# One decoder layer on one core: six pairs of weight columns multiplied by a seven-product scheme, and one projection moved

## The chip, the core and the metric

The kernel runs on one core of a Trainium2 chip. A core has TensorE (matrix products), VectorE (DVE in the profile), ScalarE (ACT), GpSimd (POOL) and SyncE (SP, which here only issues transfers). Each engine works through its own instructions in order, and engines wait for one another on semaphores. The metric is the device time of one launch, in microseconds (us).

## The reference

One layer of a hybrid decoder: 256 tokens, model width 2048, all in float32. Cut to its products:

```python
hn = rmsnorm(h, norm_mix_w)                       # h is x, (256, 2048)
q, k, v, g_ret, xr, yr, g_a, g_b = split(hn @ w_in)
ret_out = silu(g_ret) * head_groupnorm(chunkwise_retention(rotary(q), rotary(k), v))
rnn_out = gelu(yr) * rg_lru(causal_dwconv(xr))
merged = sigmoid(g_a) * (ret_out @ w_proj_ret) + sigmoid(g_b) * (rnn_out @ w_proj_rnn)
h = h + merged @ w_mix_out
h = h + memory_cross_attention(rmsnorm(h), rmsnorm(mem), xa_w_q, xa_w_k, xa_w_v) @ xa_w_o
gate, val = split(causal_dwconv(rmsnorm(h) @ ffn_w_up))
h = h + (silu(gate) * val) @ ffn_w_down           # 5632 hidden features
return rmsnorm(h, final_norm_w)
```

The matrices of the mixers and of the attention are 2048 x 2048 each (`w_in` is 2048 x 14336), `ffn_w_up` is 2048 x 11264 and `ffn_w_down` 5632 x 2048.

## The kernel before

**Units.** Every dense product is cut into *units*. A unit is one piece of a weight, 1 MB: four k-tiles of 128 rows (`KC` = 4) by 512 columns (`BW` = 512). There are 356. `weight_plan` (L64) lists the products in the order in which they are computed, `weight_stream` (L89) lays the pieces of all weights one behind the other in memory in that order ("the wall"), and `prefetch` (L191) walks along it: SP loads the next piece into one of three `raw` buffers (L202), ScalarE copies it to a rounded half `hi` (L221), VectorE subtracts to get the rest `lo` (L222). `hi` and `lo` have three buffers each, and the splits are made two units ahead. The rounding type (fp32r) lets TensorE take the product of two float32 numbers as three matmuls: high by high, low by high, high by low.

**Two kinds of product.** `gemm_t` (L253, matmuls at L276) keeps the weights stationary and gives its result by feature. `gemm_n` (L290, matmuls at L286 to L288 in `products_n`) keeps the tokens' tiles stationary and gives its result by token: two tiles of 128 tokens, four k-tiles, three matmuls of 512 columns each, so 24 in a unit. Results go to three accumulators in PSUM, each two banks (128 x 1024 float32).

**Activations** are kept by feature as `[128, 2, 512]` tiles: two k-tiles, and for each 256 tokens of the high half and 256 of the low half. `split_pair` (L330) makes them (ScalarE L337, VectorE L338), `halves` (L306) takes them apart. They and most other large tiles come from one pool of 27 buffers of 4 KB a partition (`big`); `tmp` tiles come from a second pool of ten.

**The order of the work.** q, k, v and gate of the retention; four blocks of the recurrence (`recur` L623, loop from L656); `gated` (L686) for `w_proj_rnn` four times, then for `w_proj_ret` four times, where the two are added (L705), transposed and split into `merged` (`turn_merged` L698); `residual` (L714) for `w_mix_out`; attention (`attend` L808); `residual` for `xa_w_o`; the FFN in three parts of 4, 4 and 3 blocks of 512 hidden features. In each part, `conv_up` (L834) multiplies, convolves (ScalarE L840, VectorE L842) and stores gate and value, L909 to L912 make the activation and its split `hid`, and `down` (L847) multiplies with `ffn_w_down` and adds (L853).

`residual` takes four column blocks one after the other: `gemm_n`, one VectorE add of 128 x 1024 into the residual rows `hrow` (L721), squares for the next norm, and the transposes and splits of the new rows (`turn` L727). While it multiplies `w_mix_out`, `memory_steps` (L746) does the norm of the memory rows `mnat` between the blocks.

Small work that follows a product is put off with `later(n, ...)` (L232): it is issued n units after the present one, so that TensorE has weights to multiply meanwhile. On top of that a scheduler orders the instructions of each engine when the program is built; at run time the order is fixed.

```python
for k in range(0, nk, KC):
    prefetch(1)
    (r_, c_), parts = ahead.pop(0)
    ...
    prefetch(AHEAD)
    yield k, parts
    step[0] += 1
```

Of the kernel before, what the change touches and what calls it, by code (L numbers as in the profile page):

```python
# [16 lines left out]
P = 128  # L17
# [10 lines left out]
BW = 512  # L28
# [35 lines left out]
def weight_plan():  # L64

    w0 = "w_in"
    plan = []
    for g in range(2):
        for c in (O_Q, O_K):
            plan += [(w0, 0, NT, c + g * BW), (w0, 0, NT, O_V + g * 1024 + (c == O_K) * BW)]  # L70
        plan += [(w0, 0, NT, O_G + g * 1024 + b * BW) for b in range(2)]
    for b in range(4):
        plan += [(w0, 0, NT, c + b * BW) for c in (O_XR, O_YR)]
    for c, w in ((O_GB, "w_proj_rnn"), (O_GA, "w_proj_ret")):
        for b in range(4):
            plan += [(w0, 0, NT, c + b * BW), (w, 0, NT, b * BW)]
    plan += [("w_mix_out", 0, NT, b * BW) for b in range(4)]
    plan += [(w, 0, NT, b * BW) for b in range(4) for w in ("xa_w_k", "xa_w_q")]
    plan += [(w, 0, NT, b * BW) for w in ("xa_w_v", "xa_w_o") for b in range(4)]
    b0 = 0  # L80
    for nb_ in FF_PARTS:
        for b in range(b0, b0 + nb_):
            plan += [("ffn_w_up", 0, NT, c + b * BW) for c in (0, FF)]
        plan += [("ffn_w_down", b0 * BW, 4 * nb_, b * BW) for b in range(4)]
        b0 += nb_
    return plan


def weight_stream(inputs):  # L89

    out = []
    for name, row, nk, c in weight_plan():
        w = np.asarray(inputs[name])[0]
        for k in range(0, nk, KC):
            r = row + k * P
            out.append(w[r : r + KC * P, c : c + BW].reshape(KC, P, BW).transpose(1, 0, 2))
    return np.ascontiguousarray(np.stack(out))
# [3 lines left out]
def hybrid_layer(  # L101
# [20 lines left out]
    bp = ctx.enter_context(tc.tile_pool(name="bp", bufs=27))  # L122
# [54 lines left out]
    stream = [(row + k * P, c) for w, row, nk, c in plan for k in range(0, nk, KC)]  # L177
    assert len(stream) == wall.shape[0]
# [12 lines left out]
    def prefetch(n):  # L191
        while len(ahead) < n and taken[0] < len(stream):
            row, c = stream[taken[0]]
            src = wall[taken[0]]
# [31 lines left out]
            ahead.append(((row, c), parts))  # L226
# [9 lines left out]
    def chunks(nk, w, row, c):  # L236

        w_, row_, nk_, c_ = plan[gemms[0]]
        assert (row_, nk_, c_) == (row, nk, c) and w_ == w, (gemms[0], row, nk, c)
        gemms[0] += 1  # L240
        for k in range(0, nk, KC):
            prefetch(1)
            (r_, c_), parts = ahead.pop(0)
            assert (r_, c_) == (row + k * P, c)
            prefetch(AHEAD)
            yield k, parts
# [3 lines left out]
            for _, fn in due:  # L250
                fn()

# [37 lines left out]
    def gemm_n(w, row, st, nk, col):  # L290
# [8 lines left out]
        return a  # L299

# [129 lines left out]
    def rms(rows, pin=False):  # L430

        ss = sp_.tile([P, 2, 4], F32, tag="ss0", name=nm("ss"))
        for c in range(4):
            for tt in range(2):
                junk = tp.tile([P, BW], F32, tag="tmp", name=nm("junk"))
                i = act.activation(junk, rows[c][:, tt, :], AF.Square, accum_out=ss[:, tt, c : c + 1])
                if pin:
                    tc.keep_in_program_order(i)
# [217 lines left out]
    for b in range(4):  # L656
# [28 lines left out]

    def gated(c0, w, st, b, o):  # L686

        a = gemm_n("w_in", 0, xs, NT, c0 + b * BW)
        t = tp.tile([P, 2, BW], F32, tag="sig", bufs=2, name=nm("sig"))
# [6 lines left out]
    merged = []  # L696

    def turn_merged(m, pr):  # L698
        for t in transposed(m[:, :, pr * S : (pr + 1) * S]):
            merged.append(split_pair(t, 0.5))  # L700

    mb = [gated(O_GB, "w_proj_rnn", rnn, b, big([P, 2, BW], s="mb")) for b in range(4)]
    for b in range(4):
        m = gated(O_GA, "w_proj_ret", ret, b, big([P, 2, BW], s="m"))
# [6 lines left out]
    mnat = [load_rows(mem, c) for c in range(4)]  # L711
    ms = Pairs(mem_t, p_mem)

    def residual(w, st, out, wcol, steps=None):  # L714

        ss = sp_.tile([P, 2, 4], F32, tag="ss0", name=nm("ss"))
        for b in range(4):
            if steps:
                steps(b)
            h = hrow[b]  # L720
            dve.tensor_add(h, h, gemm_n(w, 0, st, NT, b * BW))  # L721
            squares(h, ss, b)
            for pr in range(2):
                later(pr, lambda b=b, pr=pr: turn(b, pr, out, wcol))
# [21 lines left out]
    def memory_steps(b):  # L746
        if b == 1:
            rsms.append(rms(mnat))
            later(3, lambda: spread_tokens(rsms[0]))
# [6 lines left out]
    ss1 = residual("w_mix_out", merged, h1s, p_xa, memory_steps)  # L756
# [29 lines left out]
    def transpose_probs(pr_):  # L786
# [4 lines left out]
        if done[0] == len(pTs):  # L791
            two = tp.tile([P, 2, BW], F32, tag="sig", bufs=2, name=nm("pT"))
# [13 lines left out]
    osp = []  # L806

    def attend(b, v):  # L808
# [3 lines left out]
        for pr in range(2):  # L812
# [9 lines left out]
            osp.append(split_pair(oc))  # L822

# [5 lines left out]
    ss2 = residual("xa_w_o", osp, h2s, p_ffn)  # L829
# [69 lines left out]
    for part, nb_ in enumerate(FF_PARTS):  # L899
        final = part == len(FF_PARTS) - 1  # L900
        hid = []
        for b in range(b0, b0 + nb_):
# [3 lines left out]
            for pr in range(2):  # L906
# [5 lines left out]
                hid.append(split_pair(o, 0.5))  # L912
        if final:
# [8 lines left out]
        for b in range(4):  # L922
            down(b0, hid, b, final)
# [36 lines left out]
```

## Time and profile before

| | |
|---|---|
| time, median of 3 runs | 2052.53 us (2052.45, 2052.53, 2052.78) |
| span of the profiled execution | 2051.3 us; its device time is not recorded apart from the span |
| busy, share of the span | TensorE 99%, VectorE 62%, ScalarE 48%, GpSimd 0% |
| granted TensorE clock, mean | 0.999 of full speed |
| moved by DMA | 392 MB, mean 191 GB/s |
| the wall's loads of 1 MB | 353, median 4.8 us from issue to landing |

How to read what follows: in a row that groups instructions, the line of the kernel and the engine come first, then the operation, the tile written and the tiles read, the shape, the count, the busy time in us and the mean of one in ns, and then the idle time of the engine just ahead of these instructions with what ended it. In a timeline, the first two numbers are the start and the duration in us. PEld is TensorE's loading of stationary tiles, which goes on beside its matmuls. The table of windows gives, for each stretch, its length, the sum of busy time, the busy time of PE, PEld, DVE, ACT and POOL, the granted clock, the busy share of the DMA engines and their GB/s.

### The profile page before, as it was taken

To read this page: it belongs to the slowest core of one execution; us is meant where nothing else is said; L and a number is where in the kernel's file an instruction comes from. 1 tells how busy PE (TensorE), PEld (TensorE's weight loads), DVE (VectorE), ACT (ScalarE), POOL (GpSimd) and SP (SyncE) were. 2 spreads that over 40 slices of the span, in tenths; PEclk is the share of its full clock that TensorE was granted. 3 is DMA by queue.
4 is the path that set the end of the run, shared out by engine and by line. 5 is a ranking of instruction groups with operands and counts; after the bars stand their busy time and mean duration, and the time that the engine had idled before them with its cause. 6 is when DMAs were issued, how large, how long until landed. Compare 5 with 4: busy or idle time off the path is not lost.

```text
span 2051.3 us, 24956 instructions
## 1 busy us (share of the span) xinstructions
PE 2036.8 (99%) x10508; PEld 1745.5 (85%) x10508; DVE 1276.6 (62%) x1277; ACT 993.8 (48%) x1004; POOL 7.7 (0%) x12
## 2 busy tenths in 40 slices
PE   9999999999999999999999999999999999999998
PEld 7888888888888888888888888888888888888887
DVE  6747658888444454456555545577764777646765
ACT  6445437666333434455444444455543555434543
POOL 0000000000000000000000000000000000000000
PEclk9999999999999999999999999999999999999999
DMA  9554553544554544755444444545455455555453
GB/s 344 190 214 154 184 205 138 194 174 171 205 198 189 201 185 185 267 201 219 176 173 175 165 172 177 186 185 196 184 193 203 177 195 186 187 202 185 185 205 123
DMA packets 64480, 392.17 MB, mean 191 GB/s; under 512 B 7024, under 2 KB 11760, under 8 KB 19184
## 3 DMA queue, kind: packets, MB, share of 16 engines
q1 hardware_dynamic: 62848, 387.95, 50.7%
q10 hardware_dynamic: 1520, 2.63, 0.4%
q8 instruction: 82, 1.34, 0.2%
q14 instruction: 30, 0.25, 0.0%
HBM read 388.46 MB, written 2.10 MB: 190 GB/s over the span
## 4 chain that ended last, share of the span: by engine, by line
PE 94%; ACT 3%; DVE 2%; issue 1%; DMA 0%; SPq 0%; POOLq 0%; ACTq 0%
PE acc L276 42%; PE acc L286 17%; PE acc L288 17%; PE acc L287 17%; PE sm L304 2%; DVE lo L222 1%; ACT hi L221 1%; PE sm L316 1%; DVE xr L647 0%; DMA raw<-in_wall 0%; ACT aa L634 0%; ACT tt L635 0%; ACT L643 0%; DVE ti L645 0%; ACT tr L632 0%
## 5 line engine op out<-in xcount | busy, mean ns | idle before, releaser
L222 DVE TENSOR_TENSOR lo<-raw,hi 128x2048 fp32r<-128x2048 f32 (+2 forms) x360 | 815.9, 2268 | 613.3 <-ACT hi L221 613.0
L221 ACT CAST hi<-raw 128x2048 fp32r<-128x2048 f32 (+1 forms) x358 | 679.8, 1899 | 801.0 <-PE acc L287 460.9
L276 PE MATMUL acc<-s,hi 128*128 128x512 f32 x2688 | 639.6, 391 | 3.9 <-ACT hi L221 1.4
L286 PE MATMUL acc<-hi,s 128*128 128x512 f32 (+1 forms) x1528 | 591.7, 387 | 0.0
L288 PE MATMUL acc<-lo,s 128*128 128x512 f32 (+1 forms) x1528 | 590.2, 386 | 0.0
L287 PE MATMUL acc<-hi,s 128*128 128x512 f32 (+1 forms) x1528 | 590.0, 386 | 0.0
L276 PEld LDWEIGHTS acc<-s,hi 128*128 128x128 f32 x2688 | 496.1, 188 | 102.6 <-issue 3.0
L276 PEld LDWEIGHTS acc<-s,lo 128*128 128x128 f32 x2688 | 342.4, 191 | 13.0 <-DVE lo L222 1.9
L276 PE MATMUL acc<-s,lo 128*128 128x256 f32 x2688 | 350.4, 283 | 0.9 <-DVE lo L222 0.9
L288 PEld LDWEIGHTS acc<-lo,s 128*128 128x128 f32 x1528 | 287.0, 188 | 58.6 <-DVE lo L222 0.2
L287 PEld LDWEIGHTS acc<-hi,s 128*128 128x128 f32 x1528 | 287.2, 188 | 57.0 <-DVE s L338 0.2
L286 PEld LDWEIGHTS acc<-hi,s 128*128 128x128 f32 x1528 | 287.1, 188 | 56.6 <-ACT s L337 0.3
L326 ACT COPY c<-acc 128x512 f32<-128x512 f32 x84 | 48.3, 578 | 100.0 <-PE acc L276 100.0
L327 DVE TENSOR_TENSOR uz<-acc,c 128x512 f32<-128x512 f32 x44 | 30.3, 688 | 24.4 <-ACT c L326 24.4
L842 DVE SCALAR_TENSOR_TENSOR fv<-uz,pf,fv 128x255 f32<-128x255 f32 (+1 forms) x88 | 39.8, 479 | 0.0
L842 DVE SCALAR_TENSOR_TENSOR fg<-uz,pf,fg 128x255 f32<-128x255 f32 (+1 forms) x88 | 38.4, 480 | 0.0
L360 ACT ACTIVATE s<-sm,pb 128x256 fp32r<-128x256 f32 x48 | 21.8, 469 | 32.2 <-DVE s L361 31.8
L450 DVE TENSOR_TENSOR uz<-uz,rsb 128x512 f32<-128x512 f32 x44 | 30.3, 690 | 0.7
L840 ACT ACTIVATE fg<-uz,pf 128x256 f32<-128x256 f32 x44 | 25.2, 597 | 2.1 <-DVE uz L450 0.8
L361 DVE SCALAR_TENSOR_TENSOR s<-sm,pb,s 128x256 fp32r<-128x256 f32 x48 | 22.4, 480 | 5.6 <-ACT s L360 5.4
L840 ACT ACTIVATE fv<-uz,pf 128x256 f32<-128x256 f32 x44 | 25.2, 597 | 0.7
L853 DVE TENSOR_TENSOR nat<-nat,acc 128x1024 f32<-128x1024 f32 x11 | 13.4, 1221 | 18.5 <-PE acc L288 18.5
(167 smaller groups left out, 730.6 us busy)
## 6 DMA issues: line engine op xcount, KB each, us to landing
raw<-in_wall SPq DMA_DIRECT2D x353, 1024.0 KB, 4.8
raw<-in_wall SPq DMA_DIRECT2D x5, 512.0 KB, 8.3
nat<-in_x ACTq DMA_DIRECT2D x4, 512.0 KB, 10.3
nat<-in_x SPq DMA_DIRECT2D x4, 512.0 KB, 8.2
nat<-in_mem SPq DMA_DIRECT2D x4, 512.0 KB, 11.1
xt<-in_mem_t SPq DMA_DIRECT2D x8, 256.0 KB, 6.5
xt<-in_x_t SPq DMA_DIRECT2D x7, 256.0 KB, 7.8
out<-nat SPq DMA_DIRECT2D x6, 256.0 KB, 2.8
```

The source lines that it names most:

```text
L221: act.copy(hi[:, a:b], raw[:, a:b])
L222: dve.tensor_tensor(out=lo[:, a:b], in0=raw[:, a:b], in1=hi[:, a:b].bitcast(F32), op=ALU.subtract)
L276: pe.matmul(a, part, sx, start=k == 0 and t == 0, stop=k == nk - 1 and t == 0, skip_group_check=True)
L286: pe.matmul(o, h, hi, start=start, stop=False)
L287: pe.matmul(o, l, hi, start=False, stop=False)
L288: pe.matmul(o, h, lo, start=False, stop=stop)
L304: pe.matmul(o, a, b, start=start and i == 0, stop=stop and i == 2, skip_group_check=True)
L326: act.copy(c, a[:, :, S:BW])
L327: dve.tensor_tensor(out=o, in0=a[:, :, 0:S], in1=c, op=ALU.add)
L450: dve.tensor_tensor(out=z, in0=z, in1=rsb2, op=ALU.mult)
L840: act.activation(y, z[:, j, :], AF.Identity, scale=pf[:, 2, t : t + 1], bias=pf[:, 3, t : t + 1])
L842: dve.scalar_tensor_tensor(out=y[:, s:S], in0=z[:, j, 0 : S - s], scalar=pf[:, 2 - s, t : t + 1], in1=y[:, s:S], op0=ALU.mult, op1=ALU.add,)
```

## The change

**Seven products for eight.** Six times, two column blocks of 512 that follow one another (a *pair*) are no longer two calls of `gemm_n` but one call of the new `pair_add`: columns 0 and 1 of `w_mix_out` and of `xa_w_o`, and columns (0, 1) and (2, 3) of `ffn_w_down` in the first two parts of the FFN. For k-tiles 8 to 15 the products stay as they were: four units of 24 matmuls, called p. K-tiles 0 to 7 are multiplied by Strassen's scheme in Winograd's form: the two tiles of 128 tokens by the odd and the even k-tiles make a 2 x 2 matrix, odd and even k-tiles by the two column blocks make another, and seven products q1 to q7 of a quarter of the size, 12 matmuls each, take the place of eight. A pair before has 8 units of 24 matmuls, 192; after, it has 11 units, 180.

**The sums of weights.** q1, q2 and q3 read plain pieces (odd or even k-tiles of one column block). q5, q6, q7 and q4 read sums of pieces. Two `held` buffers, A and B, keep q1's and q3's pieces; q5 adds a piece to A, q7 one to B and q4 another to A by a DMA with an adding write, issued by GpSimd; q6 adds B to A on VectorE (128 x 2048). Each of the seven is split into hi and lo as before. A pair has seven plain loads of 1 MB and three accumulating ones.

**The sums of activations.** The new `sums` makes, for each of the first four stationary tiles, the four sums of 128 x 128 on VectorE, a copy on ScalarE and the split's subtraction on VectorE, at the place where these tiles are made (for `merged`, for `osp` in the attention, for `hid`).

**The adds.** In place of two VectorE adds of 128 x 1024, a pair has four of 128 x 512 and three of 128 x 1024.

**Moves.** The projection of the retention (`gated` with `w_proj_ret`) is done between block 0 and blocks 1 to 3 of the recurrence, and that of the recurrence last, where the two are added. The loads of the memory rows are issued inside the norm, which starts with the pair of `w_mix_out` rather than at its second block. The pool `big` has 25 buffers for 27, and `sig` and `pT` come from it.

```diff
+PAIR_UNITS = [
+    ("p", None, (1, 8)),
+    ("q1", "A", ("new", 0, 0)),
+    ("p", None, (1, 12)),
+    ("q3", "B", ("new", 1, 1)),
+    ("q5", "A", ("add", 0, 1)),
+    ("p", None, (0, 8)),
+    ("q6", "A", ("sum",)),
+    ("p", None, (0, 12)),
+    ("q7", "B", ("add", 0, 1)),
+    ("q2", None, ("new", 1, 0)),
+    ("q4", "A", ("add", 1, 0)),
+]
...
-            raw = wp.tile([P, KC, BW], F32, tag="raw", bufs=RAW_BUFS, name=nm("raw"))
+            if op == "new":
+                raw = wp.tile(
+                    [P, KC, BW], F32, tag="held" if slot else "raw", bufs=2 if slot else RAW_BUFS, name=nm("raw")
+                )
+                if slot:
+                    held[slot] = raw
+            else:
+                raw = held[slot]
...
-                sp.dma_start(out=raw[:, a:b, :], in_=src[:, a:b, :])
+                if op == "new":
+                    sp.dma_start(out=raw[:, a:b, :], in_=src[:, a:b, :])
+                elif op == "add":
+                    pool.dma_start(out=raw, in_=src, accum_op=ALU.add)
+                else:
+                    dve.tensor_tensor(out=raw, in0=raw, in1=held["B"], op=ALU.add)
...
+    def pair_add(w, row, st, ss, c0, c1, h0, h1):
+        xz, yv, rw = acc(), acc(), acc()
+        x, z, y, v, r, u = (t[:, i, :] for t in (xz, yv, rw) for i in range(2))
+        where = {
+            "q1": (x, "a", 0, 0), "q2": (y, "a", 1, 0), "q3": (r, "s", 3, 0), "q4": (x, "a", 1, 1),
+            "q5": (z, "s", 0, 0), "q6": (x, "s", 1, 0), "q7": (x, "s", 2, 0),
+        }
...
+        for kind, parts in units(w, row, NT, c0, c1):
+            if kind == "p":
+                k0, (a, b), (ka, kb) = ((8, (r, u), "ru"), (12, (r, u), "ru"), (8, (y, v), "yv"), (12, (y, v), "yv"))[plain]
...
+            if kind == "q1":
+                add(h0[:, 0, :], x)
+            elif kind == "q3":
+                add(h1, rw)
+            elif kind == "q5":
+                add(h1, z[:, None, :].to_broadcast([P, 2, BW]))
+            elif kind == "q6":
+                add(h1[:, 0, :], x, ALU.subtract)
+            elif kind == "q7":
+                add(h1[:, 1, :], x, ALU.subtract)
+            elif kind == "q2":
+                add(h0, yv)
+            elif kind == "q4":
+                add(h0[:, 1, :], x)
...
+    recurrent(0)
+    mb = [gated(O_GA, "w_proj_ret", ret, b, big([P, 2, BW], s="mb")) for b in range(4)]
+    for b in range(1, 4):
+        recurrent(b)
     for b in range(4):
-        m = gated(O_GA, "w_proj_ret", ret, b, big([P, 2, BW], s="m"))
+        m = gated(O_GB, "w_proj_rnn", rnn, b, big([P, 2, BW], s="m"))
...
-        for b in range(4):
-            down(b0, hid, b, final)
+        if nb_ == 4:
+            for b in (0, 2):
+                pair_add("ffn_w_down", b0 * BW, hid, hid_sums, b * BW, (b + 1) * BW, hrow[b], hrow[b + 1])
+        else:
+            for b in range(4):
+                down(b0, hid, b, final)
```

In the prediction the pairs are numbered in the order of the work: 1 is `w_mix_out`, 2 is `xa_w_o`, 3 and 4 are the first FFN part, 5 and 6 the second. The second p of a pair is the one with k-tiles 12 to 15 of the right column block.

More of the change, by code (lines that the diff above doesn't have):

```diff
@@ L251, in chunks @@
                 fn()
+    def chunks(nk, w, row, c):
+        for i, (kind, parts) in enumerate(units(w, row, nk, c)):
+            yield i * KC, parts
     def gemm_t(w, row, st, nk, col):
@@ L654, in recur, with recurrent @@
             rnn.append(split_pair(o, 0.5))
-    for b in range(4):
+    def recurrent(b):
         rgw = big([P, 2, 4, P], s="rgw")
```

173 lines of the change are left out of this document (126 added, 47 removed).

## The prediction

> **What bounds the kernel now.** I read the header of the page, then the engines' busy times, then the chain of work that ended last, then the table of windows, to see whether any stage has another limit.
>
> ```profile
> span 2051.3 us, 24956 instructions
> PE 2036.8 (99%) x10508; PEld 1745.5 (85%) x10508; DVE 1276.6 (62%) x1277; ACT 993.8 (48%) x1004; POOL 7.7 (0%) x12
> PE 94%; ACT 3%; DVE 2%; issue 1%; DMA 0%; SPq 0%; POOLq 0%; ACTq 0%
> raw<-in_wall SPq DMA_DIRECT2D x353, 1024.0 KB, 4.8
> ```
>
> TensorE is busy for 99% of the span and carries 94% of the chain; VectorE, ScalarE and the transfers have slack on average. So fewer matmuls mean less time, provided that TensorE stays fed where they are taken out. Times below are against the span of this one execution, 2051.3; the median of three runs is 2052.53, so I add 1.2 at the end.
>
> The pace comes from the timeline of TensorE at the first `down` of the FFN (its first matmul, one 21 starts later, and the one 24 starts later, which opens the next unit):
>
> ```profile
> 1490.97 0.40 PE L286 MATMUL acc<-hi,s 128*128 128x512 f32 x1
> ...
> 1495.76 0.39 PE L286 MATMUL acc<-hi,s 128*128 128x512 f32 x1
> ...
> 1496.44 0.39 PE L286 MATMUL acc<-hi,s 128*128 128x512 f32 x1
> ```
>
> From the first line to the last are 24 matmuls and 5.47 us; over longer stretches I get 0.2267 us each, so a unit p of 24 takes 5.44 us and a unit q of 12 takes 2.72. The two others work beside it, per unit:
>
> ```profile
> L222 DVE TENSOR_TENSOR lo<-raw,hi 128x2048 fp32r<-128x2048 f32 x353 | 808.4, 2291 | 610.9 <-ACT hi L221 610.7
> L221 ACT CAST hi<-raw 128x2048 fp32r<-128x2048 f32 x353 | 674.5, 1911 | 799.1 <-PE acc L287 460.9 <-issue 184.6 <-PE acc L276 132.8
> ```
>
> 1.91 for hi and then 2.29 for lo. ScalarE's idle time ends on TensorE: a split starts when the unit three back gives up its hi buffer. With units of 5.44 the pair of splits (4.2) is early; with units of 2.72 it is not.
>
> **The change, part by part.**
>
> *Matmuls.* Eight units of 24 per pair become four of 24 and seven of 12: 192 to 180. Six pairs save 72, which is 72 × 0.2267 = **16.3 us**, 2.72 a pair. All of it is on the path only if nothing below stalls TensorE.
>
> *The long accumulating transfers.* q5, q7 and q4 read a held tile after an accumulating DMA; no such transfer is in this trace. The nearest row is the plain piece of the same 1 MB above, 4.8 us, so 4.8 is the lower end (it moves at least those bytes). The accumulation also reads the held tile: two transfers' time, 9.6, is what I take, because nothing in the row says that a second read is free; three, 14.4, is the upper end. Call it D, from the moment the held tile's last reader is done until q's hi can start. [...]
>
> *Pairs 2, 4 and 6* (xa_w_o, and columns 2, 3 of the two FFN parts) keep the nominal order p q1 p q3 q5 p q6 p q7 q2 q4 on TensorE, and their stationary tiles were ready long before. With the pair's first matmul at zero, q5 starts at 5.44 + 2.72 + 5.44 + 2.72 = 16.3; hi and lo take 4.2 ahead of it, and some 1.5 of VectorE's other splits and adds stands between, so the accumulated data must be there by 10.6. The accumulation may start when lo of q1, the held tile's last reader, is done. In pair 2 that is at −3.1, so D up to 13.7 costs nothing and the pair saves 2.72. In pairs 4 and 6 q1 follows right behind short units of the pair before, and its lo ends at 2.7 only; the net is −2.72 + max(0, D − 7.9), at 9.6 **−1.0** each.
>
> *Pairs 3 and 5* (columns 0, 1 of the FFN parts). Here p's first wait is not weights but `hid`. VectorE and ScalarE in before, around the same `down`:
>
> ```profile
> 1498.48 2.28 DVE L222 TENSOR_TENSOR lo<-raw,hi 128x2048 fp32r<-128x2048 f32 x1
> 1500.68 1.66 DVE L842 SCALAR_TENSOR_TENSOR fv<-uz,pf,fv 128x255 f32<-128x255 f32 x4
> 1502.26 0.69 DVE L338 SCALAR_TENSOR_TENSOR s<-fo,s 128x512 fp32r<-128x512 f32 x1
> 1502.86 0.68 DVE L910 SCALAR_TENSOR_TENSOR fo<-ft,fg 128x512 f32<-128x512 f32 x1
> 1503.58 0.69 DVE L911 TENSOR_TENSOR fo<-fo,fv 128x512 f32<-128x512 f32 x1
> 1504.18 2.28 DVE L222 TENSOR_TENSOR lo<-raw,hi 128x2048 fp32r<-128x2048 f32 x1
> 1506.38 0.69 DVE L338 SCALAR_TENSOR_TENSOR s<-fo,s 128x512 fp32r<-128x512 f32 x1
> ```
>
> Taking 1490.97 as zero, the split of the seventh tile pair (k-tiles 12, 13) is done at 12.0 and that of the eighth (14, 15) at 16.1. In before k-tiles 12 to 15 are the fourth unit, which starts at 3 × 5.44 = 16.3: it just fits. In the changed kernel they are the second p, after p and q1 alone: 5.44 + 2.72 = 8.16. TensorE waits from 8.16 to 12.0. Then the eighth's split stands on VectorE behind q1's add (0.69), and behind lo of q5: hi and lo of q5 need the accumulation, issued at −3.0; for D up to some 14 lo ends at 16.2 by VectorE's queue alone, the last `hid` split at 16.9. p2's remaining 17 matmuls end at 20.8, q3 at 23.5, q5's last seven at 25.1, where the pace alone gives 19.04. The stall is 6.1, and the pair's net +3.4. Two such pairs: **+6.8**, whatever D is.
>
> *Pair 1* (w_mix_out). The build's order puts q5 ahead of p2 on TensorE. q5's hi takes the buffer that q1 leaves, at 8.6, so hi ends at 10.6 and lo, behind q1's add and lo of q3, at 13.0: TensorE stands about 2.1 and again 2 there. `merged`'s last split, after the DVE sum for q6, comes 0.5 late, and p3's and p4's lo, behind the adds, 1.3 and 0.85 late, from these rows:
>
> ```profile
> L721 DVE TENSOR_TENSOR nat<-nat,acc 128x1024 f32<-128x1024 f32 x8 | 9.8, 1221 | 9.7 <-PE acc L288 9.7
> L327 DVE TENSOR_TENSOR uz<-acc,c 128x512 f32<-128x512 f32 x44 | 30.3, 688 | 24.4 <-ACT c L326 24.4
> ```
>
> The pair has four adds of 0.69, three of 1.22 and the sum of 128x2048 (2.29 by the split's row) where before had two of 1.22. Stalls 6.3 less 2.72: **+3.6**, for D up to 9.8 (its accumulation starts at −1.2); beyond, one for one.
>
> *What costs nothing.* The sums for the seven products (per tile four adds of 128x128, a copy, a split) come in stages that TensorE bounds. Two of those stages, the mix and the first FFN part's end, in the table of windows (length; sum; PE, PEld, DVE, ACT, POOL; clock; DMA share; GB/s):
>
> ```profile
> 838.00:928.00 90.00, 90.00 (x416) 74.46 (x415) 51.97 (x45) 47.33 (x65) 0.70 (x1) 1.00 0.63 242
> 1490.00:1580.00 90.00, 90.00 (x402) 74.67 (x401) 50.01 (x38) 37.20 (x26) 0.00 (x0) 1.00 0.52 192
> ```
>
> TensorE is full and VectorE has 40% free. If that cover fails, about 4 × 2 us per stage show, 8 at most for one. The projections that change places, and the memory's rows that are loaded inside w_mix_out, are in stages where TensorE idles as little: from 30 to 2040 the largest waits of TensorE are
>
> ```profile
> PE acc L276 <- DVE xz L327: 1.4, 2, 0.7
> PE sm L316 <- DVE s L361: 0.6, 1, 0.6
> PE acc L276 <- DVE lo L222: 0.4, 1, 0.4
> ```
>
> The new order puts none of its own there, since each recurrent block still has a whole projection beside it. The transfers: a pair loads 10 MB for 8 in about 42 us, and a share of 0.52 to 0.63 rises to some 0.75. Two of the first pair's pieces (2 MB) go out early on SP's queue, before 55 us:
>
> ```profile
> 30.00:40.00 10.00, 10.00 (x49) 8.41 (x48) 5.18 (x4) 7.21 (x19) 0.00 (x0) 1.00 1.04 409
> 40.00:50.00 10.00, 10.00 (x47) 8.33 (x46) 8.15 (x15) 6.54 (x6) 0.70 (x1) 1.00 0.65 259
> ```
>
> The engines are full until 40, and TensorE does not idle beside them; I take 0, with 2 × 4.8 as the other end if the next unit's piece stands behind them.
>
> **The sum**, D = 9.6: 3.6 − 2.7 + 6.8 − 2.0 = **+5.7**; 2051.3 + 5.7 = 2057.0, and with 1.2 around the span **2058.2**. At D = 4.8: 3.6 − 2.7 + 6.8 − 5.4 = +2.3, 2054.8. At 14.4: 8.2 − 2.0 + 6.8 + 7.6 = +20.6, 2073.1.
>
> **The rivals.**
>
> *A, faster.* `hid` and the first accumulation come in time and TensorE never waits in the pairs: 2052.5 − 16.3 = 2036.2. It decides in pairs 3 and 5: the last `hid` split would have to be done by 8.2 after the pair's start, not by 12.0 and 16.1. For it: TensorE's short q's give VectorE less to do per matmul, and the wait may be filled by q3 or q5. Against it: the quoted timeline, and an order on TensorE that is fixed at build. If half of these stalls go, 2052.5 + 5.7 − 8 is about 2050, still on this side.
>
> *B, short accumulation.* D = 4.8: 2054.8, not to be told from no change (0.2%, 4.1 us, is what a measurement of this kernel can tell).
>
> *C, long accumulation.* D = 14.4 or more, or loads and accumulations that hold each other up: 2073 and up. For it: loads do not keep to their median when others run beside them,
>
> ```profile
> DMA to landing us min/median/max: 4.6/4.8/13.3
> nat<-in_mem SPq DMA_DIRECT2D x4, 512.0 KB, 11.1
> ```
>
> and mem's rows, half the size, took 11.1. Against it: in the pairs the share of the transfers stays under 0.8.
>
> *D, the clock.* The stalls of 3.8 in pairs 3 and 5 might lower TensorE's granted clock after them. Were it half for as long again, 1.9 us each, 3.8 in all: 2062.0. Before shows no fallen clock, even with 3.27 us of idle time in its first 10:
>
> ```profile
> 0.00:10.00 10.00, 6.73 (x32) 5.60 (x32) 4.08 (x10) 4.27 (x7) 0.20 (x4) 1.00 0.75 233
> ```
>
> [...]
>
> *Does the change do what it says?* The order on each engine of the built kernel has 12 matmuls per q unit and 18 accumulating transfers, so yes.
>
> **How the numbers follow.** My forecast, D between 7 and 12 and the stalls as worked out: 0.45. Rival A, with its halfway case: 0.17. B: 0.17. C: 0.14. D: 0.07. Faster by over 0.2% is A, 0.17; within 0.2% is B, 0.17; slower is the rest, 0.66. The range reaches from 2047, which leaves out the better part of A (0.13), to 2074, C's lower edge, which leaves out some 0.07 of C.
>
> **What would show it.** (1) The granted clock stays at 1.00 and TensorE's busy time is about 16 lower: the saving. (2) Waits of TensorE at the second p of pairs 3 and 5 on `s` (L338 in before) of some 4 us, and on q5's lo or the last `s` of 2 more: the term +6.8. (3) In pair 1 two waits of 2 us on hi and lo of q5. (4) The row of accumulating transfers: issue to landing near 9.6; then pairs 4 and 6 wait 1.7 each for it. (5) No new wait before the mix stage. It would be wrong if the build's TensorE order let q work in the waiting time, if D is far from 9.6, or if the new order of projections starves TensorE.

## The result, and the profile after

The changed kernel takes 2065.44 us (median of 4 runs, 2064.59 to 2068.96) against 2052.59 for the kernel before (2052.45 to 2052.78): a ratio of 1.0065, 95% interval 1.0051 to 1.0079. It is 12.9 us slower; 5.7 slower was forecast. The profiled run is the longest of the four, 2068.96 with a span of 2066.8, 15.5 more than the span of before. The spread has grown as well, from 0.3 us to 4.4.

The page of the changed kernel: span, engines, and the accumulating transfers (GpSimd's queue).

```profile
span 2066.8 us, 25082 instructions
PE 2034.7 (98%) x10436; PEld 1737.6 (84%) x10436; DVE 1371.5 (66%) x1411; ACT 1039.7 (50%) x1042; POOL 23.7 (1%) x30
raw<-in_wall POOLq DMA_DIRECT2D x18, 1024.0 KB, 8.8
```

TensorE has its 72 matmuls less (10508 before, 10436 now), which at 0.2267 are 16.3 us, but its busy time fell by 2.1 only. An accumulating transfer takes 8.8 us from issue to landing by the median, where 9.6 was assumed. TensorE's waits between 30 and 2040 (`s` is the split of activation tiles, L474 and L475; `hi` and `lo` that of weights, L283 and L284; `nat` a pair's add into the residual rows, L385):

```profile
PE acc L381 <- DVE s L475: 5.1, 2, 2.6
PE acc L379 <- DVE nat L385: 4.8, 2, 2.8
PE acc L382 <- DVE lo L284: 4.2, 5, 1.6
PE acc L379 <- ACT hi L283: 3.2, 1, 3.2
PE acc L379 <- ACT s L474: 1.2, 2, 0.6
```

The columns are the sum, the count and the longest. Lines 379 to 382 are the matmuls of `pair_add`, so all five rows lie in the pairs: 18.5 us of idle time where before had none. The short waits that the prediction lists for before come to 0.7, 0.6 and 0.3.

Why the busy time hardly fell is seen in the table of windows (length; sum; PE, PEld, DVE, ACT, POOL; granted clock; DMA share; GB/s). The rows are a stretch of pair 1, all of pair 2, and stretches of pair 3 and of the end of pair 4:

```profile
840.00:860.00 20.00, 15.23 (x58) 11.85 (x57) 12.53 (x10) 11.59 (x21) 1.59 (x2) 0.83 0.90 257
1222.00:1270.00 48.00, 48.00 (x224) 40.19 (x223) 36.19 (x24) 27.68 (x22) 2.46 (x3) 1.00 0.75 220
1500.00:1520.00 20.00, 16.10 (x55) 11.53 (x54) 14.23 (x15) 8.46 (x9) 0.88 (x1) 0.83 0.30 56
1580.00:1600.00 20.00, 17.22 (x84) 14.50 (x83) 13.61 (x8) 8.61 (x6) 0.00 (x0) 0.91 0.84 315
```

The granted clock is below 1.00 in the three stretches that hold a long wait or the time just behind one, and 1.00 in pair 2, which has no wait. Before, it was 1.00 from 30 to 2040. Behind pair 6's wait of 1.98 it stays at 1.00; the last section comes back to this. TensorE's timeline at the second p of pair 3 shows both losses at once:

```profile
1492.47 0.40 PE L379 MATMUL acc<-hi,s 128*128 128x512 f32 x1
...
1501.44 0.50 PE L379 MATMUL acc<-hi,s 128*128 128x512 f32 x1 [0.62 <-ACT s L474]
1504.49 0.50 PE L381 MATMUL acc<-hi,s 128*128 128x512 f32 x1 [2.55 <-DVE s L475]
...
1508.50 0.79 PE L382 MATMUL acc<-lo,ss 128*128 128x512 f32 x1 [0.68 <-DVE lo L284]
...
1509.94 0.63 PE L381 MATMUL acc<-hi,s 128*128 128x512 f32 x1
1510.37 0.63 PE L382 MATMUL acc<-lo,s 128*128 128x512 f32 x1
...
1512.50 0.45 PE L381 MATMUL acc<-hi,s 128*128 128x512 f32 x1
```

The first row is the pair's first matmul. The wait that was forecast (second p for the split of `hid`) ends at 1504.49, which is 12.0 after it. From 1505.8 to 1512.5 the clock is at half: matmuls with nothing to wait for start every 0.43 instead of every 0.23.

The pairs one by one, from the same events in both traces. VectorE's add of column 3 of `w_mix_out`, then that of `xa_w_o`, before and after:

```profile
929.30 1.22 DVE L721 TENSOR_TENSOR nat<-nat,acc 128x1024 f32<-128x1024 f32 x1 [1.39 <-PE acc L288]
...
1311.65 1.22 DVE L721 TENSOR_TENSOR nat<-nat,acc 128x1024 f32<-128x1024 f32 x1 [1.39 <-PE acc L288]
```

```profile
933.52 1.22 DVE L869 TENSOR_TENSOR nat<-nat,acc 128x1024 f32<-128x1024 f32 x1 [1.39 <-PE acc L353]
...
1313.14 1.22 DVE L869 TENSOR_TENSOR nat<-nat,acc 128x1024 f32<-128x1024 f32 x1 [1.39 <-PE acc L353]
```

The first is 4.22 late, the second 1.49: between them lies pair 2 alone, which **gave 2.7 back**. Ahead of pair 1, at VectorE's first step on the last product of the projections, the changed kernel was 1.1 early (836.75 against 837.89), so pair 1 took **5.4 more**. The FFN's second part, by the first matmul of its `down` and the first one behind it, before and after:

```profile
1755.98 0.40 PE L286 MATMUL acc<-hi,s 128*128 128x512 f32 x1
...
1843.05 1.30 PE L276 MATMUL acc<-s,hi 128*128 128x512 f32 x5
```

```profile
1765.50 0.40 PE L379 MATMUL acc<-hi,s 128*128 128x512 f32 x1
...
1858.23 1.07 PE L341 MATMUL acc<-s,hi 128*128 128x512 f32 x4
```

Pairs 5 and 6 together take 92.73 instead of 87.07, **5.7 more**. Pairs 3 and 4 began 1.50 late (1492.47 against 1490.97) and pair 5 9.52 late, so they took **8.0 more**.

### The profile page after: what moved, and what is told of

The parts are those of the page before. It is cut to its first block, busy times and chain, and to the rows that moved or that the text cites. A ratio compares the mean times of both kernels' runs of the same rounds, so it can differ in the third digit from the quotient of the medians.

```text
span 2066.8 us, 25082 instructions
## 1 busy us (share of the span) xinstructions
PE 2034.7 (98%) x10436; PEld 1737.6 (84%) x10436; DVE 1371.5 (66%) x1411; ACT 1039.7 (50%) x1042; POOL 23.7 (1%) x30
## 4 chain that ended last, share of the span: by engine, by line
PE 51%; DMA 3%; DVE 3%; issue 1%; ACT 1%; POOLq 0%; ACTq 0%; DVEq 0%
PE acc L341 32%; PE acc L353 4%; PE acc L351 4%; PE acc L352 4%; DMA raw<-in_wall 3%; PE acc L382 2%; PE acc L381 2%; PE acc L379 2%; DVE lo L284 2%; PE sm L441 1%; ACT hi L283 1%; PE sm L453 0%; DVE fv L993 0%; DVE nat L385 0%; DVE fo L1061 0%
## 5 line engine op out<-in xcount | busy, mean ns | idle before, releaser
L284 DVE TENSOR_TENSOR lo<-raw,hi 128x2048 fp32r<-128x2048 f32 (+2 forms) x378 | 856.7, 2268 | 554.4 <-ACT hi L283 553.7
L283 ACT CAST hi<-raw 128x2048 fp32r<-128x2048 f32 (+1 forms) x376 | 713.0, 1899 | 750.9 <-PE acc L352 298.7
L351 PE MATMUL acc<-hi,s 128*128 128x512 f32 (+1 forms) x1144 | 442.2, 387 | 0.0
L353 PE MATMUL acc<-lo,s 128*128 128x512 f32 (+1 forms) x1144 | 441.1, 386 | 0.0
L352 PE MATMUL acc<-hi,s 128*128 128x512 f32 (+1 forms) x1144 | 440.8, 385 | 0.0
L353 PEld LDWEIGHTS acc<-lo,s 128*128 128x128 f32 x1144 | 214.9, 188 | 43.8 <-DVE lo L284 0.6
L352 PEld LDWEIGHTS acc<-hi,s 128*128 128x128 f32 x1144 | 215.1, 188 | 42.0 <-DVE s L475 0.2
L351 PEld LDWEIGHTS acc<-hi,s 128*128 128x128 f32 x1144 | 215.1, 188 | 42.0 <-ACT s L474 0.3
L379 PE MATMUL acc<-hi,s 128*128 128x512 f32 x264 | 105.9, 401 | 6.1 <-DVE nat L385 4.8
L381 PE MATMUL acc<-hi,s 128*128 128x512 f32 x264 | 105.0, 398 | 5.1 <-DVE s L475 5.1
L382 PE MATMUL acc<-lo,s 128*128 128x512 f32 x264 | 105.0, 398 | 1.3 <-DVE lo L284 1.3
L379 PEld LDWEIGHTS acc<-hi,s 128*128 128x128 f32 x264 | 50.9, 193 | 19.7 <-issue 5.6
L381 PEld LDWEIGHTS acc<-hi,s 128*128 128x128 f32 x264 | 51.0, 193 | 16.4 <-DVE s L475 5.7
L382 PEld LDWEIGHTS acc<-lo,s 128*128 128x128 f32 x264 | 50.7, 192 | 12.9 <-DVE lo L284 2.1
L379 PE MATMUL acc<-hi,ss 128*128 128x512 f32 x96 | 39.5, 411 | 3.2 <-ACT hi L283 3.2
L382 PE MATMUL acc<-lo,ss 128*128 128x512 f32 x96 | 39.0, 409 | 3.0 <-DVE lo L284 3.0
```

Source lines behind the costliest of these rows:

```text
L283: act.copy(hi[:, a:b], raw[:, a:b])
L284: dve.tensor_tensor(out=lo[:, a:b], in0=raw[:, a:b], in1=hi[:, a:b].bitcast(F32), op=ALU.subtract)
L351: pe.matmul(o, h, hi, start=start, stop=False)
L352: pe.matmul(o, l, hi, start=False, stop=False)
L353: pe.matmul(o, h, lo, start=False, stop=stop)
L379: pe.matmul(o, h, hi, start=key not in begun, stop=False, skip_group_check=True)
```

## The experiments

The theory after the result has three parts: the saving of 16.3 is whole; TensorE stalls because of late activation splits in pairs 3 and 5 and late accumulations elsewhere; and the idle time lowers TensorE's clock. The rivals: the accumulating transfers alone are the cost; VectorE's queue is; the projections in their new place cost something; the matmuls are slow because of the transfers.

### Pair 2 alone

```diff
-    plan += residual_plan("w_mix_out")
+    plan += [("w_mix_out", 0, NT, b * BW) for b in range(4)]
...
-        if nb_ == 4:
+        if False:
```

> Seven products in pair 2 (xa_w_o) alone, the other five pairs as before; projections in the new order. Theory (the saving is whole where nothing waits, the new order costs nothing): 2.7 less than before, 2049.8. Rival, the new order of projections or the smaller pool costs something that the other terms hid: 2051 or more; rival, a pair saves less than its matmuls: 2051 to 2052.5.

Measured: 2049.74, 2.9 less than before (2052.65), ratio 0.9986 (0.9977 to 0.9995). That bears out two terms: a pair in which nothing waits saves its matmuls, and the projections in their new order cost nothing.

### Without the adding

```diff
-                    pool.dma_start(out=raw, in_=src, accum_op=ALU.add)
+                    pool.dma_start(out=raw, in_=src)
```

> The 18 accumulating transfers become plain ones from the same queue into the same held tiles: the weight sums by DMA are left out, bytes read from memory and all waits stay. Changed kernel: 2065.4, with TensorE waits of 4.8 in pair 1, 3.9 in pairs 3 and 5, 3.4 and 2.6 in pairs 4 and 6, and 12.7 of matmuls at half clock. Theory (late activation splits in pairs 3 and 5, transfers only elsewhere): landing falls from 8.8 to about 5; the waits in pairs 4 and 6 and half of that in pair 1 go with some of the slow matmuls, those of pairs 3 and 5 stay as they are: about 2057 (2054 to 2060). Rival, the long accumulations are the whole cost: every wait goes, about 2037 to 2042.

Measured: 2054.39, 1.7 above before (ratio 1.0008, 0.9999 to 1.0017) and 11 less than the change, at the lower end of what was expected. The same 1 MB from the same queue lands in 5.1 without the add, and the waits are

```profile
raw<-in_wall POOLq DMA_DIRECT2D x18, 1024.0 KB, 5.1
PE acc L381 <- DVE s L475: 5.1, 2, 2.6
PE acc L382 <- DVE lo L284: 2.6, 3, 1.6
PE acc L379 <- ACT hi L283: 1.3, 1, 1.3
PE acc L379 <- ACT s L474: 1.2, 2, 0.6
```

The row for the add `nat` (4.8 before this edit: the last q of pairs 4 and 6) is gone and pair 1's wait for hi fell from 3.2 to 1.3. The two rows for `s`, in pairs 3 and 5, are unchanged to the tenth: that wait has nothing to do with the accumulations, as the prediction said.

### Second and third p exchanged

```diff
     ("q1", "A", ("new", 0, 0)),
-    ("p", None, (1, 12)),
+    ("p", None, (0, 8)),
     ("q3", "B", ("new", 1, 1)),
     ("q5", "A", ("add", 0, 1)),
-    ("p", None, (0, 8)),
+    ("p", None, (1, 12)),
...
```

The add that takes q3's accumulator moves too: it now stands behind the third p.

> Second and third p of a pair change places, so that k-tiles 12 to 15 of the activations are first wanted 16 to 19 us after the pair's start and not after 8.2. Theory (the activation splits come too late): the waits of pairs 3 and 5 go, 3.9 each, and with them the slow matmuls behind them, 3.8 each: 15 less, 2050; pair 1 may give 2 to 6 more, since TensorE no longer takes q5 ahead of p2: 2044 to 2050. Rival, the accumulations are the cost: the waits move to q5 and the time stays at 2062 to 2066.

Measured: 2058.33, ratio 1.0025 (1.0015 to 1.0036): 7 less than the change, half of what the theory asked for. The waits:

```profile
PE acc L379 <- DVE nat L385: 12.4, 7, 3.2
PE acc L382 <- DVE lo L284: 2.8, 2, 1.6
```

The waits for `s` (6.3) are gone, and so is pair 1's for hi (3.2). But the row for `nat` grew from 4.8 to 12.4: with TensorE no longer held up early in the pair, the later accumulations are what comes last (the next run, without adding, bears that out). A wait was taken away and another stood behind it.

### Both

> The exchange of the second and third p, and the 18 accumulating transfers plain (weight sums by DMA left out, as in the run without adds). Theory (late activation splits and long accumulations are all that stalls TensorE): no wait but one of 1.6 in pair 1, the clock stays up, 2052.6 - 16.3 + 2 to 4 = 2037 to 2041. Rival, VectorE's order in the pairs stalls TensorE by itself: 2044 or more.

Measured: 2037.32, ratio 0.9925 (0.9910 to 0.9940), 15.4 less than before. Its span, engines and all of its waits between 30 and 2040:

```profile
span 2034.9 us, 25091 instructions
PE 2022.7 (99%) x10436; PEld 1733.5 (85%) x10436; DVE 1371.5 (67%) x1411; ACT 1039.9 (51%) x1042; POOL 17.6 (1%) x30
PE acc L341 <- DVE xz L464: 0.7, 1, 0.7
PE sm L453 <- DVE s L498: 0.6, 1, 0.6
PE acc L341 <- DVE lo L284: 0.3, 1, 0.3
```

No wait in any pair is left; even the 1.6 that was expected to stay is gone. VectorE has the same 1371.5 of work as in the change, so its queue is no limit by itself. The span is 16.4 under that of before: the whole saving of 72 matmuls. And it gives the account of the change: with the same 10436 matmuls TensorE is busy for 2022.7 here and for 2034.7 in the change, so **12.0 us are matmuls at a lower clock**; 18.5 are waits; together 30.5 of the 31.9 between the two spans. The granted clock says the same: in the profiled run of the change it is at half for 6.8, 6.8, 3.4 and 6.8 us in pairs 1, 3, 4 and 5, 23.9 in all, and here never between 30 and 2030.

### Holes in the kernel before

```diff
         a = gemm_n("w_in", 0, xs, NT, c0 + b * BW)
...
+        c = tp.tile([P, 8, 2], F32, tag="hu", bufs=1, name=nm("hu"))
+        act.copy(c[:, 0, :], a[:, 1, 0:2])
+        for i in range(n):
+            pool.tensor_tensor(out=c[:, i + 1, :], in0=c[:, i, :], in1=mhalf[:, 0:2], op=ALU.mult)
+        t = small()
+        tc.keep_in_program_order(pe.matmul(t[:, 0, 0:2], ones, c[:, n, :], start=True, stop=True))
         z = gemm_n(w, 0, st, NT, b * BW)
```

> The kernel before, with eight holes for TensorE and nothing else: in each of the eight projections of the mixers, the first matmul waits for a copy and a chain of 0, 1, ... 7 small GpSimd operations on the product before it (its values aren't used). Estimated holes 0.7 + 0.9 k, about 30 in all, no accumulating transfer. Theory (idle time by itself lowers the clock): holes under 2 are followed by matmuls at 0.227 each, holes over 3 by 3 to 7 us of matmuls at about 0.43; 2052.6 + 30 + 6 to 16 = 2088 to 2098. Rival, slow matmuls come from the accumulating transfers or the full queues in the pairs: none behind any hole, 2082.

Measured: 2114.48, ratio 1.030; the mean clock is 0.986. The holes were longer than estimated and closer together in length, 4.1 to 5.8 us and 39.8 in all, so the short end that was to show a threshold is missing. All eight are followed by 7 to 12 matmuls at 0.43. The shortest and the longest, with the end of the slow stretch:

```profile
563.36 0.59 PE L317 MATMUL sm<-hu,ones 128*128 128x2 f32 x2 [4.14 <-POOL hu L315]
...
568.22 0.47 PE L289 MATMUL acc<-hi,s 128*128 128x512 f32 x1
```

```profile
875.34 0.59 PE L317 MATMUL sm<-hu,ones 128*128 128x2 f32 x2 [5.78 <-POOL hu L315]
...
878.92 0.42 PE L289 MATMUL acc<-hi,s 128*128 128x512 f32 x1
```

This kernel has no accumulating transfer and no pair, and the DMA engines are busy for 0.3 to 0.6 of the time there. So idle time alone brought the half clock in this run, and the longer hole is not followed by the longer slow stretch (7 matmuls after 5.78, 10 after 4.14). In both the granted clock is at half for 6.83 us (561.53 to 568.36, 872.14 to 878.97), but a part of that lies in the hole itself.

The traces agree on the pace at half clock (0.43 a matmul against 0.227) and on its length (3.41 or 6.83 us, whatever the length of the hole). No single length of wait marks what is enough: two waits of 0.62 and 2.55 with a matmul between them brought it in pair 3 of the change, and a single one of 1.93 in pair 3 of the kernel with the p's exchanged.

### The holes of pairs 3 and 5 filled

```diff
             if kind == "q1":
                 add(h0[:, 0, :], x)
+                if w == "ffn_w_down" and c0 == 0:
+                    t = small().rearrange("p a n -> p (a n)")
+                    hi = parts[0][0][:, 0, :]
+                    for i in range(12):
+                        pe.matmul(t, halves(st[4], 0, slice(0, P))[0], hi, start=True, stop=True)
```

> Twelve matmuls of 512 columns with a result that nothing reads stand between q1 and the second p in pairs 3 and 5 (2.7 us each at full pace), where TensorE waits 3.9; no wait is taken away. Theory (the clock falls because TensorE idles): the idle time shrinks to about 1.2 per pair, the clock stays up, and the slow matmuls, 3.8 per pair, go: 7 to 8 less with more work, about 2058. Rival, the matmuls are slow for another reason (contention with the transfers, say): 2065 or, where the filling doesn't fit into the wait, up to 2068.

Measured: 2069.13 (2063.68 to 2071.24, ratio 1.0075, 1.0061 to 1.0089), 3.7 more than the change. The forecast of 2058 failed. In the profiled run (2068.05) the waits for `s` fell from 6.3 to 2.5 and the time at half clock from 23.9 to 13.7, with none left in pair 5. But the waits for `nat` grew from 4.8 to 5.8 and brought half clock behind pair 6, the idle time that the filling left still lowered the clock in pair 3, and 24 matmuls (5.4 at full pace) had to be paid. So the clock went as the theory had it and the time did not, and by the time alone this run does not decide between theory and rival. Between the four runs the mean clock was 0.994 to 0.997 and the time went with it. Matmuls for nothing are no remedy here.

### Earlier chains, other sums

What was left behind the exchanged p's is a chain in every pair: accumulation (q5), VectorE sum (q6), accumulation (q4). Three steps on it, each on top of the exchange. First, q1 ahead of the first p, and the two held buffers changing roles from pair to pair:

```diff
+    ("q1", "A", ("new", 0, 0)),
     ("p", None, (1, 8)),
-    ("q1", "A", ("new", 0, 0)),
...
+                turn_ = (pairs[0] + (slot == "B")) % 2
                 raw = wp.tile(
-                    [P, KC, BW], F32, tag="held" if slot else "raw", bufs=2 if slot else RAW_BUFS, name=nm("raw")
+                    [P, KC, BW], F32, tag=f"held{turn_}" if slot else "raw", bufs=1 if slot else RAW_BUFS,
...
```

> On top of the exchange of the second and third p (2058.3, whose waits are 7 at the last q's, 12.4 in all, on the add that stands behind a late accumulation): q1 comes first in a pair, and the two held buffers change their roles from pair to pair, so that q1's piece loads into the buffer that q7 of the pair before gave back. The chain accumulation, sum, accumulation may start some 4 to 5.4 earlier in each pair. Theory (what is left is that chain): the waits of up to 3.2 go and with them the slow clock behind them; with one wait of 1.6 left in pair 1, 2052.6 - 16.3 + 1 to 5 = 2038 to 2042. Rival, two accumulations at a time hold each other up, so an earlier start lands hardly earlier: 2050 to 2056. Rival, VectorE's queue in a pair is full and is the limit: 2046 to 2052.

Measured: 2053.17, ratio 1.0002 (0.9993 to 1.0011): 5 less, where 16 to 20 was hoped for. The time lies in the first rival's range, and the last accumulation is again issued while q7's is under way, in five of six pairs, and needs 11.8 to 12.6. But pair 4, with the 12.6, has hardly a wait left (0.4). Of the 8.4 us of waits for `nat`, 7.7 lie in pairs 3 and 5, on q6's add and on q7's; both stand on VectorE behind lo of a unit whose accumulation has just landed, q7's after 8.1, q4's after 12.0. So the chain as a whole is late there, and not only its last transfer. The pattern is easiest to see in the changed kernel, at the end of pair 4:

```profile
1565.12 12.92 DMA raw<-in_wall
...
1578.15 1.92 ACT hi L283
...
1582.30 0.69 DVE nat L385
```

hi of q4 starts 0.1 after the landing; lo of q4 (1580.09) stands on VectorE ahead of q7's add (1582.30), and q4 needs that add's accumulator. So the wait is booked on `nat`, and the 12.92 us transfer is its cause: VectorE, idle for 3.94 ahead of lo of q4, took q7's add only behind it, and TensorE waited 2.78.

Second, q4's sum by a plain load and a VectorE add; in pairs 3 and 5 q2 also comes ahead of q7:

```diff
...
+                elif op == "vadd":
+                    sp.dma_start(out=raw, in_=src)
+                    dve.tensor_tensor(out=held[slot] if KEEP[kind] else raw, in0=raw, in1=held[slot], op=ALU.add)
...
```

> On top of q1 first (2053.2; its waits are on the adds of q6 and q7 that stand on VectorE behind lo of a unit whose accumulation is late, 8.4 in all; 12.6 for an accumulation beside another, 8.1 alone): q4's sum is made by a plain load and one VectorE add (2.3), so 12 accumulating transfers are left and no two are under way at once; in pairs 3 and 5 q2 comes ahead of q7. Theory (the chain of two accumulations is what is left): the waits at q4 go, at q7 of pairs 3 and 5 some 1.2 stay, in pair 1 about 2; 2037.3 (no accumulation at all) + 3 to 8 = 2040 to 2045. Rival, VectorE is the limit in a pair (one more operation of 2.3 in some 41): 2048 to 2055.

Measured: **2047.66**, ratio 0.9976 (0.9967 to 0.9986), 5.0 under the kernel before and 17.8 under the change, though 3 more than the theory allowed. The waits:

```profile
PE acc L403 <- DVE nat L409: 6.2, 3, 2.9
PE acc L406 <- DVE lo L308: 1.1, 1, 1.1
```

With 12 accumulations, none beside another, the longest takes 9.7. The two waits of 2.9 and 2.6 are q4 behind q7 in pairs 3 and 5, longer than the 1.2 that I had put there; the first is followed by 3.4 us of half clock, the second is not.

Third, all three sums on VectorE:

> On top of q1 first: q5's, q7's and q4's sums all by a plain load and a VectorE add of 2.3 each; no accumulating transfer is left. VectorE has then some 41 of work in a pair of 41 by the durations seen (11 splits of 2.29, four such sums, adds of 6.5) and more in pairs 3 and 5. Theory (the accumulations' latency is what stalls): no wait but what VectorE's queue makes; where it is full, 1 to 3 a pair: 2040 to 2055. Rival, VectorE saturates and every pair takes as long as before or longer: 2053 to 2070.

Measured: 2050.65, ratio 0.9989 (0.9981 to 0.9998). No accumulation is left, and no half clock either (1.00 from 30 to 2040), yet the kernel is 3 us slower than the second step. The waits in the pairs, on lo and hi of the units, are many and short (nine, 8.4 in all, the longest 2.0). In pair 2 VectorE is busy for 36.0 of 43.6 us and TensorE never waits. In the two FFN parts it is busy for 79.4 of 87.4 and 79.7 of 86.2, and these pairs take about as long as before (87.1), as the rival had it. So the sums on VectorE cost nothing in pair 2, where it has room, and take up the saving in the FFN parts, where it has not.

A mixture, with q7's sum on VectorE in pairs 3 and 5 only and q2 back between q7 and q4:

> As the run with q4's sum on VectorE (2047.7), but in pairs 3 and 5 q7's sum is made on VectorE too, and q2 stands between q7 and q4 again: the one wait of 2.9 and 2.6 there (q4 for the add of q7 just ahead) is gone, short ones of 0.9 (seen where all sums are on VectorE: 2.0 in all, none followed by slow matmuls) come instead; the accumulation stays where VectorE has no room. Theory: 2047.7 - 5.5 + 4 - 1 to 2 of slow clock = 2043 to 2046. Rival, pairs 4 and 6 pay for it (q1's split late): 2047 to 2050.

Measured: 2047.54, ratio 0.9978 (0.9969 to 0.9986): no better than the second step. The waits of 2.9 and 2.6 went, but pairs 4 and 6 got 1.0 and 1.9 instead, in the pairs that the rival named, though not at q1: TensorE waits there for q6's add. The short waits of 0.9 are there too, two in each of pairs 3 and 5.

### The change, with q4's sum alone on VectorE

> The changed kernel (2065.4) with one edit: q4's sum by a plain load and a VectorE add instead of an accumulation beside q7's. Order of units as in the change. Theory (in pairs 4 and 6 the accumulation of 12 to 13 that lies beside another is what stalls q4): the waits of 2.8 and 2.0 there and the slow matmuls behind them (1.6) go, pairs 1, 3 and 5 stay: 2058 to 2061. Rival, the waits at q4 come from VectorE's order (q7's add behind lo of q4) and stay whatever the transfer: 2064 to 2067.

Measured: 2059.64, ratio 1.0040 (1.0027 to 1.0054), 5.8 less than the change and in the expected range. But the expected reason does not carry it. Pair 4's wait of 2.8 and pair 6's of 2.0 went, and others came in their place, some 3.0 in each of the two pairs:

```profile
PE acc L390 <- DVE lo L292: 6.8, 7, 1.5
PE acc L389 <- DVE s L483: 5.1, 2, 2.6
PE acc L387 <- ACT hi L291: 3.5, 1, 3.5
PE acc L387 <- DVE nat L393: 1.4, 2, 0.8
```

The idle time in the pairs is about the same, 18.0; it lies in shorter pieces, and the matmuls behind them in pair 4 run at full pace. TensorE's busy time fell from 2034.7 to 2031.2 with the same matmuls, 3.5 of the 5.5 between the two spans: most of the gain is the clock's, by these two profiled runs. Half clock lasts 13.7 us here against 23.9, and it is 3.4 less in each of pairs 3, 4 and 5. In pairs 3 and 5 the waits for `s` are the same as in the change, so that part is not what the edit was to do. Four of its five other runs (2059.1 to 2059.7) gain as much against the change at mean clocks that hardly differ (0.995 to 0.996 against 0.995), so how the gain divides stays open: the number came as expected, the mechanism is not shown.

## Why the prediction was right in sign and less than half in size

**The saving, 16.3: right.** 16.4 by the spans of before and of the kernel without waits.

**Pair 2, −2.7: right**, by the traces and by the run with that pair alone (−2.9, with the projections moved).

**The order of the projections, the sums of activations, the early loads, 0: right.** The run with pair 2 alone shows the first, and none of the kernels has a wait outside the pairs that the kernel before did not have.

**Pairs 3 and 5: the stall right, the clock behind it missing.** The second p waited for the split of `hid` to 12.0 after the pair's start, to the tenth as read off the trace of before. The second stall, for lo of q5, ended at 16.0 (1508.50), where 16.2 was forecast. TensorE's idle time is 3.9 a pair and not 6.1 only because matmuls at half clock, from 1505.79 on, filled part of it. What the sum lacked is the half clock behind that point, up to 1512.61: 4.1 us at half, an estimated 2 us a pair. It was priced at nothing in the forecast. For the two FFN parts the forecast had 6.8 − 2.0 = +4.8; they cost 13.7, and what is not in these 2 us a pair lies in pairs 4 and 6.

**Pair 1: the wrong reason, and the clock missing.** +3.6 was forecast and 5.4 measured: 4.8 of idle time (6.3 in the forecast, for parts that add up to 6.75), and 6.8 us at half clock, 3.4, which was not in the sum. I had q5 wait for the buffer of hi that q1 leaves, at 8.6 after the start, that is 845.2. The chain shows the transfer instead:

```profile
835.66 11.27 DMA raw<-in_wall
...
847.03 1.91 ACT hi L283
```

The accumulation, beside the loads of x's and mem's rows (4 MB, issued from 830.3 to 834.8), took 11.3 where I had 9.6, and without the adds the wait shrank from 3.2 to 1.3.

**D, 9.6: right by the median (8.8), wrong as one number.** In the change it is 8.0 to 8.9 alone, 11.3 beside the loads of rows, and 11.1 to 12.9 when issued while another accumulation is under way. I had the accumulation for q5 as the one that matters in pairs 4 and 6 (1.7 each). It was in time; the late one is q4's (waits of 2.8 and 2.0), since it starts only after accumulation, sum and split, with q7's under way. That chain was not in the sum at all. The lower end, 4.8 by the plain piece from SP's queue, is too low: from GpSimd's queue it is 5.1 without the add and 8.8 with it. That the add costs a second transfer's time was an estimate; by these two numbers it costs 3.7, 0.7 of one.

**The clock: the step that failed.** Rival D had a chance of 0.07 and 3.8 us; the loss is 12.0 in the profiled run, the largest miss in the sum. Half clock for as long again as the stall was an assumption of mine: the runs show the half (0.43 a matmul against 0.227), but for 3.41 or 6.83 us, here 6.83 behind the waits of 0.62 and 2.55 in pair 3. I let the row of the first 10 us speak against it (3.27 idle at 1.00). That row can't: its idle time is in pieces of 1.05 to 1.15, and its first matmuls (L173) start every 0.21 us up to 3.98 and every 0.11 from there: they ran at half pace at first, which the row's 1.00 does not show. And I priced it for two places where there were four (pairs 1, 3, 4 and 5). So: 18.5 of waits against some 22 foretold, plus 12.0, less 16.3, makes +14.2; the spans differ by 15.5. By the median of all runs it is 12.9: the profiled run is the longest, with a mean clock of 0.993 where the three others have 0.995, by which the clock costs them an estimated 4 us less (0.002 of 2066).

**Rival A, faster**, was to be decided in pairs 3 and 5 alone. The exchange of two units shows that it isn't: without those waits the time is still above that of before, because q4's chain stands behind.

## What to carry to other kernels

Where TensorE is full, count a stall twice: for its length, and for the matmuls at half clock that may follow it, here 12.0 us for 18.5 of waits in the profiled run. Units that get shorter bring every later need forward, so check for each operand (the activations, not the weights alone) when it is ready against when it is now wanted, and follow each chain of transfer, sum and transfer to the end of the stage, with two adding transfers beside each other priced as such (in the change 11.1 to 12.9 for the second, 8.0 to 8.9 for one alone). An order that takes late operands late, and a sum on an engine with room in place of the last transfer in the chain, made of a loss of 12.9 a gain of 5.0. The rest to 15.4 was not got: with transfers that add it goes into waits for them, with all sums on VectorE into waits for VectorE.

## What the runs showed of the hardware

An adding write of 1 MB from GpSimd's queue into SBUF took 8.8 us by the median (the change), a plain one of the same bytes from the same queue 5.1 (the run without the adding), and one from SP's queue 4.8 (both). Where a second adding one was issued while the first was under way, three times in the change, the second took 11.1, 12.9 and 12.1, and the first 8.9 to 9.2; with q1 first the longest took 12.6.

The length of a wait alone did not say whether half clock followed. Waits of 1.93 (pair 3 with the p's exchanged), 2.8 (pair 4 of the change) and 2.9 were followed by it; 2.6 (pair 5 with q4's sum on VectorE) and 2.0 (pair 6 of the change) were not. What decides, as far as these traces show it, is seen in the moments at which the granted clock changes: within one run they lie a whole number of 3.41 us apart. In the change it falls to half at 850.43, 1505.79, 1584.29 and 1778.85, which are 192, 23 and 57 times 3.413 apart, and in the kernel with holes it rises again at 568.36 and 878.97, 91 times. Here are such stretches of the change, around the waits of pairs 3 and 6, in the columns of the table of windows:

```profile
1502.37:1505.79 3.42, 1.29 (x6) 0.89 (x6) 3.42 (x8) 1.33 (x1) 0.00 (x0) 1.00 0.00 0
1505.79:1509.20 3.41, 2.69 (x6) 1.36 (x6) 3.41 (x4) 0.63 (x1) 0.00 (x0) 0.50 0.00 0
1509.20:1512.61 3.41, 3.41 (x10) 2.64 (x9) 2.05 (x1) 0.00 (x0) 0.70 (x1) 0.50 0.02 5
1512.61:1516.02 3.41, 3.41 (x17) 2.78 (x16) 0.00 (x0) 0.95 (x1) 0.18 (x1) 1.00 0.82 127
...
1853.94:1857.36 3.42, 1.97 (x9) 1.65 (x10) 3.42 (x3) 1.98 (x2) 0.00 (x0) 1.00 0.06 24
1857.36:1860.77 3.41, 3.41 (x17) 2.82 (x16) 3.41 (x4) 1.92 (x1) 0.00 (x0) 1.00 0.71 211
```

The stretch in which TensorE idles for 2.1 us is followed by one at half clock, the one with 1.4 is not. The stretch at half clock with 0.7 of idle time is followed by another, the one without idle time by full clock. Cut in this way between 30 and 2030, the thirteen traces have 26 stretches at full clock with 1.92 or more of idle time, and half clock follows all of them; of eight with 1.50 to 1.87 it follows two; with 1.49 or less none. Of 42 stretches at half clock, the 28 with 0.60 or less of idle time are the last ones, and the 14 with 0.68 or more are not. So half clock lasted 3.41 or 6.83 us in these traces, and a wait of 2 to 3 us brought it or not by where it fell in these stretches, which differs from trace to trace.

Kernels with such holes differ from run to run by up to 9 us (2059.08 to 2068.01 for the change with q4's sum on VectorE), and the longest of these has the lowest mean clock (0.994 against 0.995 and 0.996), though the clock does not account for all of the difference; the kernel without waits in its pairs differs by 0.5.
